# A two-layer encoder on one Trainium2 core: pair products in another order and other bank places, low keys in one tile, weights split in halves, and vector and scalar work held to its order of issue

## The chip, the cores and the metric

The kernel runs on one NeuronCore of a Trainium2 chip. TensorE (PE) multiplies, VectorE (DVE), ScalarE (ACT) and GpSimd (POOL) do the rest, and SyncE (SP) and POOL issue DMAs. Each engine works through its own queue in order; semaphores between queues make one engine wait for another. The metric is the device time of one execution in microseconds (us), lower being better, as the median of three runs.

## The reference

The reference is an encoder trunk of two layers on 512 tokens of width 1024, in float32. Layer 0 is windowed attention with a SwiGLU block, and the diff leaves it alone. Layer 1 is the part that matters here:

```python
def dilated_mixture_attention(h, w_qkv, w_out):
    b, s, _ = h.shape
    qkv = (h @ w_qkv).reshape(b, s, N_GROUPS_B, 3, H_B, HEAD_DIM)
    slopes = alibi_slopes(H_B)[:, None]
    outs, lses = [], []
    for gi, (win, dil) in enumerate(DILATED_GROUPS):
        q = to_residue(qkv[:, :, gi, 0], dil)[:, :, :, None]
        k = to_residue(qkv[:, :, gi, 1], dil)
        v = to_residue(qkv[:, :, gi, 2], dil)
        o, lse = banded_attention(q, k, v, slopes, dil, win // (2 * dil), BLOCK_B)
        outs.append(from_residue(o[:, :, :, 0], b, dil))
        lses.append(from_residue(lse[:, :, :, 0], b, dil))
    wts = jax.nn.softmax(jnp.stack(lses), axis=0)
    o = jnp.einsum('gbsh,gbshd->bshd', wts, jnp.stack(outs).astype(jnp.float32))
    return o.astype(h.dtype).reshape(b, s, H_B * HEAD_DIM) @ w_out
```

It has 16 heads of width 64 in three groups (windows 128, 512 and 2048 with steps 1, 4 and 16), and all queries, keys and values come from one product of the normalised input with `w_qkv`.

## The kernel before

**Precision.** A product of two float32 matrices is made of three matmuls in a reduced float32 type (fp32r): both operands are split into a high part, which ACT copies (`wh`, `xh`, `oh`), and a low part, which DVE subtracts (`wl`, `xl`, `ol`); then high x high, high x low and low x high are added up in a PSUM bank.

**Layer 1** works through pairs of heads, `p` from 0 to 7. For groups 1 and 2 (and group 0 from pair 1 on), the query and key projections of a pair are made together by a scheme of Strassen's kind with seven products instead of eight: `pair_unit(p, g)`. Each product is 12 matmuls of 128 x 128 weights against 256 columns; the line records two half products of six. The products are numbered 1 to 7. Products 1, 2 and 7 run against the normalised input (`xh`, `xl`), the others against sums of it (`oh`, `ol`). Weights 1 and 2 are the two halves of a loaded tile, 6 and 4 those of a tile of sums, and 5, 7 and 3 lie in the buffers `slots`. A unit uses two PSUM banks, `a` and `b`, and in each the halves `one` and `two`. Before, products 1, 5, 6 and 3 pile up in `a[one]`: each adds to what lies there, and between them ACT or DVE reads the place out: after 1 and 5 the gate copies of L1300, after 4 and 3 copies into the keys (L1308, L1314), after 6 an add into the keys (L1311), after 7 the queries (L1318 or L1122).

**Values.** `in_order_values` (group 0) and `value_pair` (groups 1 and 2) make the values. For the first, `value_weights` loads two weight tiles and splits each whole (L115 on ACT, L116 on DVE).

**Attention.** For group 0, `parts(p)` splits queries and keys of a pair. A head's queries `qs[a]` hold the high part in its own 64 partitions and the low part in the other 64. Its keys `ks[a]` hold the high part twice, and `kl[a]` the low part twice (the second time by an ACT copy, L163). `scores_a` then runs for each of two blocks and two heads a matmul with `ks[a]` and one with `kl[a]`, both over 128 partitions: eight matmuls a call, two calls a pair. `scores_b` makes the scores of groups 1 and 2 with 64 partitions a head, the two heads side by side on the array (L1515). `weigh_a` and `weigh_b` weigh the values, in 64 columns a head.

**Order.** PE's order is the order in which the program is written. For ACT and DVE a scheduler sets the order, by readiness as it estimates it. `paced` writes the program of this part: it walks a line of half products (`fill`, made by `lined`) and, at places given by number, issues the steps of attention (`even`, `odd` and their variants for pairs 0 and 1), of normalising the input for the products (`normed`, `operand`, `summed`) and of writing x away (`parked`). `lined` issues the preparations of each unit (loads, sums, splits) at offsets in half products from the unit's first one.

Of the kernel before, what the change touches and what calls it, by code (L numbers as in the profile page):

```python
# [14 lines left out]
S = 512  # L15
# [64 lines left out]
def trunk(ctx, tc, xT, gains, sink, tabs, qsc, wunits, wv, outT, outR):  # L80
# [1014 lines left out]
    with tc.tile_pool(name="l1", bufs=2) as pool:  # L1095
# [102 lines left out]
        def in_order_values(pg):  # L1198
            w, loads, halves = value_weights(1 + 3 * pg)

            def gen():
                if pg:
                    v = pool.tile([128, 4, 256], F32, name="va", bufs=3)
                else:
                    slots["w"] = const.tile([128, NK - 2, S], F32R, name="slots", tag="xb")
                    v = const.tile([128, 4, 256], F32, name="va", tag="xa")
                vals[pg, 0] = v
                yield from v_products(oh, ol, w, v, "ov sc tp mm".split() if pg == 1 else ["mm"] * 4,
                                      lambda b: norm["r"][:, b:b + 1])

            return 16, gen(), [(-11, loads), (-3, lambda: halves(0)), (-2, lambda: halves(1))]

        def pair_unit(p, g):
# [23 lines left out]

            def high(names, src):
                t[names] = [wpool.tile([128, 1024], F32R, name=n) for n in ("wh", "wl")]
                nc.scalar.activation(t[names][0], t[src], AF.Copy)  # L1240

            def low(names, src):
                h, l = t[names]
                nc.vector.tensor_tensor(l, t[src], h.bitcast(F32), op=OP.subtract)
                for k, m in enumerate(names):
                    w[m] = tiles(*[z[:, 512 * k:512 * k + 512] for z in (h, l)])

# [18 lines left out]
            preps = [(-26, sums), (-16, raw), (-8, lambda: high((1, 2), "raw")), (-7, lambda: low((1, 2), "raw")),  # L1266
                     (-5, lambda: add(5)), (-4, lambda: high_one(5)), (-3, lambda: low_one(5)),
                     (-2, lambda: high((6, 4), "sums")), (-1, lambda: low((6, 4), "sums")),
                     (0, lambda: add(7)), (-2, last), (2, lambda: high_one(7)), (3, lambda: low_one(7)),
                     (4, lambda: high_one(3)), (5, lambda: low_one(3))]  # L1270

# [26 lines left out]

            def copied(h):
                nc.scalar.activation(o["gate"][:, (one, two)[h]], o["a"][:, one], AF.Copy, scale=nqs)  # L1300
# [6 lines left out]
            def done4():  # L1307
                nc.scalar.activation(half(o["second"], 1), src(o["b"][:, two]), AF.Copy)  # L1308

            def done6():  # L1310
                nc.vector.tensor_tensor(half(o["second"], 1), src(o["a"][:, one]), half(o["second"], 1), op=OP.add)  # L1311

            def done3():
                nc.scalar.activation(half(o["second"], 0), src(o["a"][:, one]), AF.Copy)  # L1314

# [13 lines left out]
            after = [] if g else list(zip((15, 17, 24, 26), parts(p)))  # L1329
            return 14, products(), preps + after  # L1330

        def value_pair(pg):
# [34 lines left out]
            for m, a in ((1, -5), (2, -2), (5, 2), (4, 6), (6, 10), (7, 14), (3, 18)):  # L1367
                preps += [(a, lambda m=m: high(m)), (a + 1, lambda m=m: low(m))]
            preps += [(1, lambda: add(5)), (9, lambda: add(7))]

# [60 lines left out]
        def scores_a(p, ts):  # L1431
# [6 lines left out]
            for t in ts:  # L1438
                o = tile_a(t)[0]
                for a in range(2):  # L1440
                    out, kp = ps[a][:, o:o + 256], [qk[n, p][a] for n in ("ks", "kl")]
                    if t == 0:
# [5 lines left out]
                    for k in range(2):  # L1448
                        nc.tensor.matmul(out, qk["qs", p][a][:, 128 * t:128 * t + 128], kp[k],  # L1449
                                         start=t == ts[0] and k == 0, stop=k == 1, skip_group_check=True)  # L1450
# [230 lines left out]

        def paced(n, steps, done=0):

            for at, step in sorted((s for s in steps if done <= s[0] < n or s[0] == n == starts[8]), key=lambda s: s[0]):
                spread([at - done, step], fill)
                done = at
            spread([n - done], fill)

# [56 lines left out]
        def x_back():  # L1745
            nonlocal x
            x = stream()
            for j in range(NK):
# [3 lines left out]
                "x01": 43, "x23": 45, "r01": 46, "r23": 48, "back": 57}  # L1752
        odd = {"a01": -12, "xa01": -9, "a23": -8, "xa23": -5, "merge": -4, "t01": 5, "t23": 12, "group": 28,
               "x01": 31, "x23": 37, "r01": 35, "r23": 41, "back": 51}
# [4 lines left out]
        line += [(at, lambda j=j: summed(j)) for j, at in enumerate((50, 52, 54, 56))]  # L1759
        line += [(64 + at, lambda j=j: operand(j)) for at, j in enumerate((4, 5, 6, 7, 0, 1, 2, 3))]  # L1760
        starts = [sum(counts[:p + 1]) for p in range(9)]
        for p in range(8):
            ats = even if p % 2 == 0 else odd
            if p == 0:
                ats = {"a01": -47, "xa01": -44, "a23": -31, "xa23": -28, "merge": -22, "t01": 36, "t23": 44, "group": 56,
                       "x01": 59, "x23": 61, "r01": 63, "r23": 65, "back": 71}
            elif p == 1:
                ats = {**odd, "a01": 13, "xa01": 15, "a23": 16, "xa23": 18, "merge": 19, "t01": 22, "t23": 26}
            steps = attention(p)
# [97 lines left out]
```

## Time and profile before

| | us |
|---|---|
| median of three runs | 1355.34 (1354.69 to 1355.9) |
| the profiled execution, whole | 1357.63 |
| its span, first to last instruction | 1355.8 |
| mean granted TensorE clock | 0.996 |

The value products of layer 1 begin near 522 us and the pair units near 590; the output projection takes over near 963. In the profile's rows, `mm` and `psv` are PSUM banks for products, `sc` for scores, `ov` and `ovb` for weighed values, `tp` for transposes. A row of the timeline has its start, its length, the engine, the line, the operation with the tiles written and read, its shape, the count, and in brackets the engine's idle time before it with what ended it. Successive matmuls overlap: a row of 0.28 us may have its successor start 0.11 us later, so what a matmul takes from the stream is read from the starts. A shape such as 64*128 says that 64 rows and 128 columns of the array are used.

### The profile page before, as it was taken

To read this page: it belongs to the slowest core of one execution; us is meant where nothing else is said; L and a number is where in the kernel's file an instruction comes from. 1 tells how busy PE (TensorE), PEld (TensorE's weight loads), DVE (VectorE), ACT (ScalarE), POOL (GpSimd) and SP (SyncE) were. 2 spreads that over 40 slices of the span, in tenths; PEclk is the share of its full clock that TensorE was granted. 3 is DMA by queue.
4 is the path that set the end of the run, shared out by engine and by line. 5 is a ranking of instruction groups with operands and counts; after the bars stand their busy time and mean duration, and the time that the engine had idled before them with its cause. 6 is when DMAs were issued, how large, how long until landed. Compare 5 with 4: busy or idle time off the path is not lost.

```text
span 1355.8 us, 29663 instructions
## 1 busy us (share of the span) xinstructions
PE 1335.4 (98%) x11874; PEld 1314.5 (97%) x11874; DVE 1071.1 (79%) x1901; ACT 814.5 (60%) x1477; POOL 291.7 (22%) x393
## 2 busy tenths in 40 slices
PE   9999999999999999999999999999999999999997
PEld 9988999999999999998999999999999999999997
DVE  6776558877879999778888788788566887878985
ACT  6776544555555568657777677677444555555553
POOL 1233330121211001023314314313131021210104
PEclk9999999999999999999999999999999999999998
DMA  6110262688765447285556656655245388774821
GB/s 209 63 63 17 78 176 84 178 205 205 185 161 153 135 149 204 71 205 140 148 148 157 151 146 157 155 142 141 102 134 155 111 214 204 187 189 133 199 74 63
DMA packets 86122, 196.36 MB, mean 145 GB/s; under 512 B 11104, under 2 KB 13536, under 8 KB 85984
## 3 DMA queue, kind: packets, MB, share of 16 engines
q1 hardware_dynamic: 63136, 153.42, 35.6%
q0 software_dynamic: 22560, 40.52, 18.3%
q8 instruction: 93, 1.52, 0.5%
q10 hardware_dynamic: 288, 0.52, 0.1%
q14 instruction: 45, 0.37, 0.1%
HBM read 188.59 MB, written 5.84 MB: 143 GB/s over the span
## 4 chain that ended last, share of the span: by engine, by line
PE 82%; ACT 8%; DVE 6%; issue 2%; DMA 1%; POOL 0%; DVEq 0%; SPq 0%; ACTq 0%; POOLq 0%
PE mm L761 18%; PE sc L761 14%; PE mm L144 14%; PE mm L1285 12%; PE psv L144 6%; PE tp L144 6%; PE sc L144 2%; ACT pr L1536 2%; PE ov L467 1%; PE ov L144 1%; DMA w<-wunits 1%; PE sc L1449 1%; ACT pr L443 1%; PE mm L998 1%; DVE pr L436 1%
## 5 line engine op out<-in xcount | busy, mean ns | idle before, releaser
L717 POOL DMA_DIRECT2D w<-wunits x92 | 80.8, 920 | 445.8 <-DMA w<-wunits 145.7
L116 DVE TENSOR_TENSOR wl<-wraw,wh 128x1024 fp32r<-128x1024 f32 (+4 forms) x92 | 98.3, 1078 | 20.9 <-ACT wh L115 18.4
L115 ACT ACTIVATE wh<-wraw 128x1024 fp32r<-128x1024 f32 (+4 forms) x91 | 83.1, 928 | 50.4 <-PE mm L144 40.3
L761 PE MATMUL mm<-bh,wh 128*128 128x256 f32 x368 | 101.6, 276 | 0.0
L761 PE MATMUL mm<-bl,wh 128*128 128x256 f32 x368 | 101.6, 276 | 0.0
L761 PE MATMUL mm<-bh,wl 128*128 128x256 f32 x368 | 101.6, 276 | 0.0
L761 PE MATMUL sc<-bh,wh 128*128 128x256 f32 x368 | 101.6, 276 | 0.0
L761 PE MATMUL sc<-bl,wh 128*128 128x256 f32 x368 | 101.6, 276 | 0.0
L761 PE MATMUL sc<-bh,wl 128*128 128x256 f32 x368 | 101.6, 276 | 0.0
L761 PE MATMUL mm<-bh,h 128*128 128x256 f32 x368 | 101.6, 276 | 0.0
L761 PE MATMUL mm<-bl,h 128*128 128x256 f32 x368 | 101.6, 276 | 0.0
L761 PE MATMUL mm<-bh,l 128*128 128x256 f32 x368 | 101.6, 276 | 0.0
L144 PE MATMUL mm<-xh,wh 128*128 128x256 f32 x384 | 78.3, 286 | 0.4 <-ACT xh L280 0.4
L1285 PE MATMUL mm<-oh,slots 128*128 128x256 f32 x368 | 74.0, 284 | 2.0 <-ACT ssum L1300 1.6
L144 PE MATMUL mm<-xl,wh 128*128 128x256 f32 x384 | 76.0, 280 | 0.0
L144 PE MATMUL mm<-xh,wl 128*128 128x256 f32 x384 | 75.9, 279 | 0.0
L144 PE MATMUL psv<-wl,oh 128*128 128x256 f32 x256 | 72.0, 281 | 2.2 <-DVE wl L116 2.2
L144 PE MATMUL psv<-wh,oh 128*128 128x256 f32 x256 | 72.3, 282 | 0.7 <-ACT v L1393 0.6
L144 PE MATMUL psv<-wh,ol 128*128 128x256 f32 x256 | 71.7, 280 | 0.0
L761 PEld LDWEIGHTS sc<-bl,wh 128*128 128x128 f32 x368 | 69.1, 188 | 0.0
L761 PEld LDWEIGHTS mm<-bl,h 128*128 128x128 f32 x368 | 69.1, 188 | 0.0
L761 PEld LDWEIGHTS mm<-bh,wl 128*128 128x128 f32 x368 | 69.1, 188 | 0.0
(348 smaller groups left out, 5146.8 us busy)
## 6 DMA issues: line engine op xcount, KB each, us to landing
wraw<-wunits SPq DMA_DIRECT2D x122, 512.0 KB, 4.0
w<-wunits SPq DMA_DIRECT2D x207, 256.0 KB, 4.0
w<-wunits POOLq DMA_DIRECT2D x138, 256.0 KB, 6.4
wraw<-wv SPq DMA_DIRECT2D x21, 512.0 KB, 4.6
wraw<-wunits SPq DMA_DIRECT2D x16, 384.0 KB, 4.4
w<-wv SPq DMA_DIRECT2D x8, 512.0 KB, 3.6
w<-wv POOLq DMA_DIRECT2D x8, 512.0 KB, 7.6
xb<-xT SPq DMA_DIRECT2D x6, 256.0 KB, 5.4
```

Source lines behind the costliest of these rows:

```text
L115: nc.scalar.activation(out_h, src, AF.Copy)
L116: nc.vector.tensor_tensor(out_l, src, out_h.bitcast(F32), op=OP.subtract)
L144: nc.tensor.matmul(out[:, cols], a, b[:, cols], start=first and k == 0 and c == 0, stop=last and k == 2, skip_group_check=True)
L436: nc.vector.tensor_tensor_reduce(out=pr[:, e, :w], in0=ps[hf], in1=tab0[:, off:off + w], scale=SLOPES[heads[e]], scalar=-3e38, op0=OP.add, ...
L443: nc.scalar.activation(pr[:, e, :w + 1], pr[:, e, :w + 1], AF.Exp, bias=m[:, 1, e:e + 1], accum_out=m[:, 2, e:e + 1])
L467: nc.tensor.matmul(ov[64 * hf:64 * hf + 64, 256 * n:256 * n + 256], v0[:, k0 // 128 + kb, vs], st["pt", kb][:, 256 * hf:256 * hf + 256], s ...
L717: nc.gpsimd.dma_start(sums[:, 512 * k:512 * k + 512], v[:, 0:512], accum_op=OP.add)
L761: nc.tensor.matmul(out, a[:, j], b[:, j], start=first and j == 0 and i == 0, stop=j == 3 and i == 2, skip_group_check=True)
L998: nc.tensor.matmul(ps[:, 256 * h:256 * h + 256], a, (bl if low else bh)[:, slot, q % 4], start=q == 4 and k == 0 and 256 * h == cols.start ...
L1285: nc.tensor.matmul(out, a[:, j], b[:, j], start=first and j == 0 and i == 0, stop=j == 3 and i == 2, skip_group_check=True)
L1449: nc.tensor.matmul(out, qk["qs", p][a][:, 128 * t:128 * t + 128], kp[k], start=t == ts[0] and k == 0, stop=k == 1, skip_group_check=True)
L1536: nc.scalar.activation(of(pr[:, a, :], c), of(pr[:, a, :], c), AF.Exp, bias=nm[:, c % 2, a:a + 1], accum_out=den[:, c % 2, a:a + 1])
```

## The change

**Keys.** `kl` becomes one tile. Each head's low part stays in its own 64 partitions, the ACT copy L163 goes, and the second matmul of each pair in `scores_a` runs over those 64 partitions, against the high half of the queries alone: the product of the two low parts is left out. In the program the matmul then takes the array as 64 by 128, and the one before and after it as 128 by 128.

```diff
-                    qk["kl", p] = [pool.tile([128, S], F32R, name=f"kl{a}", bufs=1) for a in range(2)]
-                split_keys(qk["k", p, 0], qk["ks", p], qk["kl", p], (a,))
+                    qk["kl", p] = pool.tile([128, S], F32R, name="kl", bufs=1)
+                own, other = (HALVES, HALVES[::-1])[a]
+                k, hi = qk["k", p, 0], qk["ks", p][a]
+                nc.scalar.activation(hi[own], k[own], AF.Copy)
+                nc.scalar.activation(hi[other], hi[own].bitcast(F32), AF.Copy)
+                nc.vector.tensor_tensor(qk["kl", p][own], k[own], hi[own].bitcast(F32), op=OP.subtract)
...
-                    out, kp = ps[a][:, o:o + 256], [qk[n, p][a] for n in ("ks", "kl")]
+                    out, kp = ps[a][:, o:o + 256], [qk["ks", p][a], qk["kl", p][HALVES[a]]]
+                    qp = [qk["qs", p][a], qk["qs", p][a][HALVES[a]]]
...
-                        nc.tensor.matmul(out, qk["qs", p][a][:, 128 * t:128 * t + 128], kp[k],
+                        nc.tensor.matmul(out, qp[k][:, 128 * t:128 * t + 128], kp[k],
```

PE at the first scores of layer 1, before (`psv` is the value product around them):

```order
L144 MATMUL psv<-wh,ol 128x256
L1449 MATMUL sc<-ks_6723,qs_6714 128x256
L1449 MATMUL sc<-kl_6725,qs_6714 128x256
L1449 MATMUL sc<-ks_6724,qs_6715 128x256
L1449 MATMUL sc<-kl_6726,qs_6715 128x256
```

And now:

```order
L144 MATMUL psv<-wh,ol 128x256
L1459 MATMUL sc<-ks_6731,qs_6722 128x256
L1459 MATMUL sc<-kl,qs_6722 128x256
L1459 MATMUL sc<-ks_6732,qs_6723 128x256
L1459 MATMUL sc<-kl,qs_6723 128x256
```

The order is the same; the two `kl` rows read a 64-partition half of one tile each.

**Pair units.** The products run 1, 5, 2, 4, 6, 7, 3 instead of 1, 2, 5, 4, 6, 7, 3. Product 1 goes to `b[two]` and is read by two ACT copies (gate and keys), product 5 opens `a[one]`, 2 goes to `b[one]`, 4 and 7 add to `b[two]`, 6 and 3 to `a[one]`. The copy after product 3 becomes a DVE add.

```diff
             def done1():
                 o["first"], o["second"] = new_q(p, g), new_k(p, g)
                 o["gate"] = o["first"] if g else spool.tile([128, S], F32, name="ssum", bufs=1)
-                copied(0)
+                scaled(0, "b", two)
+                kept(0, "b", two)
...
-                for gen in (product(1, "a", one, True, done1), product(2, "b", one, True, lambda: None),
-                            product(5, "a", one, False, lambda: copied(1)), product(4, "b", two, False, done4),
-                            product(6, "a", one, False, done6), product(7, "b", two, False, done7),
-                            product(3, "a", one, False, done3)):
+                for gen in (product(1, "b", two, True, done1),
+                            product(5, "a", one, True, lambda: scaled(1, "a", one)),
+                            product(2, "b", one, False, lambda: None),
+                            product(4, "b", two, False, lambda: kept(1, "b", two)),
+                            product(6, "a", one, False, lambda: added(1, "a", one)),
+                            product(7, "b", two, False, done7),
+                            product(3, "a", one, False, lambda: added(0, "a", one))):
```

ACT behind the first weighing of values, where the unit of pair 1 and group 0 begins (`acca` is the weighed values, `ssum` the gate copy, `ka` the keys, `mb` and `pr` the exponentials of `scores_b`), before:

```order
L1502 ACTIVATE acca<-ov 128x512
L1536 ACTIVATE pr_7833,mb<-pr_7833,mb 128x2x128 x4
L1300 ACTIVATE ssum<-mm,qs_sb 128x256
L1538 ACTIVATE mb<-mb 128x4
L1536 ACTIVATE pr_7851,mb<-pr_7851,mb 128x2x128 x4
L1538 ACTIVATE mb<-mb 128x4
L1300 ACTIVATE ssum<-mm,qs_sb 128x256
```

And now:

```order
L1512 ACTIVATE acca<-ov 128x512
L1546 ACTIVATE pr_7845,mb<-pr_7845,mb 128x2x128 x4
L1308 ACTIVATE ssum<-mm,qs_sb 128x256
L1311 ACTIVATE ka<-mm 128x8x32
L1548 ACTIVATE mb<-mb 128x4
L1546 ACTIVATE pr_7863,mb<-pr_7863,mb 128x2x128
L1308 ACTIVATE ssum<-mm,qs_sb 128x256
```

Four exponentials still stand ahead of the first gate copy. The key copy follows it at once, and the second gate copy has moved ahead of three more exponentials.

**Weights.** The splits of the tiles of products 1 and 2 and of 6 and 4 are made in halves of 512 columns (`high` and `low` with a half `k`), at offsets of their own.

```diff
-            def high(names, src):
-                t[names] = [wpool.tile([128, 1024], F32R, name=n) for n in ("wh", "wl")]
-                nc.scalar.activation(t[names][0], t[src], AF.Copy)
+            def high(names, src, k):
+                if names not in t:
+                    t[names] = [wpool.tile([128, 1024], F32R, name=n) for n in ("wh", "wl")]
+                cols = slice(512 * k, 512 * k + 512)
+                nc.scalar.activation(t[names][0][:, cols], t[src][:, cols], AF.Copy)
...
-            return 16, gen(), [(-11, loads), (-3, lambda: halves(0)), (-2, lambda: halves(1))]
+            return 16, gen(), [(-15, loads), (-7, lambda: halves(0)), (-2, lambda: halves(1))]
```

**Order of issue.** `paced` now marks, after each half product, the newest ACT and the newest DVE instruction, and what is issued from the third half product on may not be ordered ahead of the mark on its engine. Some offsets of attention steps change too (for odd pairs `merge` from -4 to 0, `x01` from 31 to 34, `x23` from 37 to 39, and a few of pairs 0 and 1).

```diff
+            for c in range(n + 1):
+                with ExitStack() as held:
+                    for mark in marks[c - 3] if c >= 3 else ():
+                        held.enter_context(tc.issue_after(mark))
+                    for step in at.get(c, ()) if c < n else [f for s, f in steps if s == n == starts[8]]:
+                        step()
+                    if c < n:
+                        next(fill)
+                marks.append([newest(e) for e in (mybir.EngineType.Activation, mybir.EngineType.DVE,)])
```

DVE during the group 0 values, from the low half of one unit's first weight tile on (`wl` are the low halves of value weights, L1711 and its successor L1732 normalise the input, L1717 to L1719 make sums of it), before:

```order
L116 TENSOR_TENSOR wl<-wraw,wh 128x1024
L1711 SCALAR_TENSOR_TENSOR v_6667<-xb,g_sb,rb 128x512
L1711 SCALAR_TENSOR_TENSOR v_6668<-xb,g_sb,rb 128x512 x2
L1717 TENSOR_TENSOR k_6661<-k_6661 128x256
L116 TENSOR_TENSOR xl<-v_6667,xh 128x512 x2
L116 TENSOR_TENSOR xl<-v_6668,xh 128x512 x2
L1718 TENSOR_TENSOR k_6661<-v_6667,k_6661 128x256
L1717 TENSOR_TENSOR k_6662<-k_6662 128x256
L1719 SCALAR_TENSOR_TENSOR v_6667<-k_6661,v_6667 128x256
L116 TENSOR_TENSOR wl<-wraw,wh 128x1024
```

And now:

```order
L116 TENSOR_TENSOR wl<-wraw,wh 128x1024
L116 TENSOR_TENSOR xl<-v_6667,xh 128x512
L116 TENSOR_TENSOR wl<-wraw,wh 128x1024
L1732 SCALAR_TENSOR_TENSOR v_6667<-xb,g_sb,rb 128x512
L1468 ISA pr_7003,mx_7012<-sc,tab_6509 128x256
```

The second subtraction follows the first after one other row; before, three rows of normalising, four low parts and four sums stood between them.

More of the change, by code (lines that the diff above doesn't have):

```diff
@@ L1236, in tiles, with low @@
                 return [z.rearrange("p (j c) -> p j c", j=4) for z in (h, l)]
-            def high(names, src):
-                t[names] = [wpool.tile([128, 1024], F32R, name=n) for n in ("wh", "wl")]
[L1240 to L1246, printed above, removed]
+            def high(names, src, k):
[3 more added lines that the diff above has]
+                nc.scalar.activation(t[names][0][:, cols], t[src][:, cols], AF.Copy)
+            def low(names, src, k):
+                h, l = [z[:, 512 * k:512 * k + 512] for z in t[names]]
+                nc.vector.tensor_tensor(l, t[src][:, 512 * k:512 * k + 512], h.bitcast(F32), op=OP.subtract)
+                w[names[k]] = tiles(h, l)
             def one_of(m):
@@ L1264, in add @@
                 nc.vector.tensor_tensor(out, t["sums"][:, 512:1024] if m == 5 else one_of(5)[2], out, op=OP.add)
[L1266 to L1270, printed above, removed]
+            first, later = ((1, 2), "raw"), ((6, 4), "sums")
+            preps = [(-26, sums), (-16, raw), (-8, lambda: high(*first, 0)), (-7, lambda: low(*first, 0)),
+                     (-7, lambda: add(5)), (-6, lambda: high_one(5)), (-4, lambda: low_one(5)),
+                     (-4, lambda: high(*first, 1)), (-3, lambda: low(*first, 1)), (-1, lambda: add(7)),
+                     (-2, lambda: high(*later, 1)), (-1, lambda: low(*later, 1)),
+                     (-1, lambda: high(*later, 0)), (-1, lambda: low(*later, 0)),
+                     (-2, last), (2, lambda: high_one(7)), (3, lambda: low_one(7)),
+                     (2, lambda: high_one(3)), (3, lambda: low_one(3))]
             def against(m):
@@ L1297, in src, with scaled, kept, added @@
                 return of_class(z, 8) if g == 0 else z
-            def copied(h):
-                nc.scalar.activation(o["gate"][:, (one, two)[h]], o["a"][:, one], AF.Copy, scale=nqs)
+            def scaled(h, key, cols):
+                nc.scalar.activation(o["gate"][:, (one, two)[h]], o[key][:, cols], AF.Copy, scale=nqs)
+            def kept(h, key, cols):
+                nc.scalar.activation(half(o["second"], h), src(o[key][:, cols]), AF.Copy)
+            def added(h, key, cols):
+                nc.vector.tensor_tensor(half(o["second"], h), src(o[key][:, cols]), half(o["second"], h), op=OP.add)
             def done1():
@@ L1304, in done1 @@
                 o["gate"] = o["first"] if g else spool.tile([128, S], F32, name="ssum", bufs=1)
-                copied(0)
[L1307 to L1314, printed above, removed]
+                scaled(0, "b", two)
+                kept(0, "b", two)
             def done7():
@@ L1368, in value_pair @@
                 preps += [(a, lambda m=m: high(m)), (a + 1, lambda m=m: low(m))]
-            preps += [(1, lambda: add(5)), (9, lambda: add(7))]
+            preps += [(1, lambda: add(5)), (8, lambda: add(7))]
             def product(m, key, first, post):
@@ L1680, in lined, with newest, paced @@
                 yield
[L1682 to L1687, printed above, removed]
+        def newest(engine):
+            return next(i for i in reversed(nc.cur_bb.bb.instructions) if i.engine == engine)
+        def paced(n, steps):
+            at, marks = {}, []
+            for c, step in sorted(steps, key=lambda s: s[0]):
+                at.setdefault(max(c, 0), []).append(step)
+            for c in range(n + 1):
[7 more added lines that the diff above has]
+                marks.append([newest(e) for e in (mybir.EngineType.Activation, mybir.EngineType.DVE,)])
         norm["by class"] = pool.tile([128, S], F32, name="acca", bufs=1)
@@ L1752, in trunk @@
                 "x01": 43, "x23": 45, "r01": 46, "r23": 48, "back": 57}
-        odd = {"a01": -12, "xa01": -9, "a23": -8, "xa23": -5, "merge": -4, "t01": 5, "t23": 12, "group": 28,
-               "x01": 31, "x23": 37, "r01": 35, "r23": 41, "back": 51}
+        odd = {"a01": -12, "xa01": -9, "a23": -8, "xa23": -5, "merge": 0, "t01": 5, "t23": 12, "group": 28,
+               "x01": 34, "x23": 39, "r01": 35, "r23": 41, "back": 51}
         ats, line, begin = [], [], 0
@@ L1758, in trunk @@
         line += [(at, lambda j=j: normed(j)) for j, at in enumerate((18, 20, 22, 24, 26, 35, 37, 39))]
-        line += [(at, lambda j=j: summed(j)) for j, at in enumerate((50, 52, 54, 56))]
-        line += [(64 + at, lambda j=j: operand(j)) for at, j in enumerate((4, 5, 6, 7, 0, 1, 2, 3))]
+        line += [(at, lambda j=j: summed(j)) for j, at in enumerate((50, 52, 55, 56))]
+        line += [(63 + at, lambda j=j: operand(j)) for at, j in enumerate((4, 5, 6, 7, 0, 1, 2, 3))]
         starts = [sum(counts[:p + 1]) for p in range(9)]
@@ L1764, in trunk @@
             if p == 0:
[L1765 to L1766 removed]
+                ats = {"a01": -45, "xa01": -44, "a23": -31, "xa23": -28, "merge": -22, "t01": 34, "t23": 44, "group": 56,
+                       "x01": 59, "x23": 61, "r01": 63, "r23": 65, "back": 68}
             elif p == 1:
[L1768 removed]
+                ats = {**odd, "a01": 13, "xa01": 15, "a23": 16, "xa23": 18, "merge": 19, "t01": 19, "t23": 28}
             steps = attention(p)
```

2 lines of the change are left out of this document (1 added, 1 removed).

## The prediction

> **What bounds the kernel now.** I read the page's busy times and chain first, then the stretch table around the part that the diff touches, then the waits of TensorE there.
>
> ```profile
> span 1355.8 us, 29663 instructions
> ...
> PE 1335.4 (98%) x11874; PEld 1314.5 (97%) x11874; DVE 1071.1 (79%) x1901; ACT 814.5 (60%) x1477; POOL 291.7 (22%) x393
> ...
> PE 82%; ACT 8%; DVE 6%; issue 2%; DMA 1%; POOL 0%; DVEq 0%; SPq 0%; ACTq 0%; POOLq 0%
> ...
> 522.00:590.00 68.00, 65.76 (x561) 65.32 (x560) 55.61 (x99) 43.47 (x79) 7.22 (x11) 0.97 0.44 122
> 590.00:980.00 390.00, 383.93 (x3655) 375.29 (x3655) 319.14 (x726) 271.46 (x602) 111.02 (x152) 1.00 0.59 150
> ```
>
> TensorE bounds it, with 98% of the span. The last two rows are the value products (522 to 590 us) and the pair units with attention (590 to 980); columns are PE, PEld, DVE, ACT and POOL busy, then clock and DMA. DVE works 319 of 390 us there and ACT 271, so neither is full; they matter only where TensorE waits for one instruction of theirs. These are all such waits from 519 to 985 us (total idle, times, longest):
>
> ```profile
> PE mm L1285 <- ACT q L1300: 2.7, 5, 0.6
> PE psv L144 <- DVE wl L116: 2.2, 2, 1.9
> PE mm L1285 <- ACT ssum L1300: 1.6, 4, 0.5
> PE sc L1449 <- DVE sta L1461: 0.7, 1, 0.7
> PE psv L144 <- ACT v L1393: 0.6, 2, 0.3
> ```
>
> So 7.8 us of idle time is what another order could win at the most directly. A wait costs more than its idle time, as one of the four ssum waits shows:
>
> ```profile
> 619.48 0.49 ACT L1536 ACTIVATE pr<-pr,mb 128x256 f32<-128x256 f32 x1
> ...
> 619.97 0.45 ACT L1300 ACTIVATE ssum<-mm,qs_sb 128x256 f32<-128x256 f32 x1
> ...
> 619.81 0.28 PE L1285 MATMUL mm<-xh,wl 128*128 128x256 f32 x1
> 620.48 0.38 PE L1285 MATMUL mm<-oh,slots 128*128 128x256 f32 x1 [0.39 <-ACT ssum L1300]
> 620.70 0.28 PE L1285 MATMUL mm<-ol,slots 128*128 128x256 f32 x1
> ```
>
> Product 5 adds into the place that product 1 left and ACT must first copy out; ACT does the exponentials before that copy. The matmuls start 0.67 and then 0.22 us apart, where undisturbed ones start 0.115 apart (rows below). That is 0.66 us lost for 0.39 shown, so 0.27 more than the view says: the restart.
>
> **Term 1, pair units: minus 6.7 us.** Now product 5 opens a bank place of its own, product 4 follows product 1 with two products between, and product 6 follows 5 with two between instead of one. The nine L1300 waits are those of 5 for the first copy and of 6 for the second. Two products are 24 matmuls, 2.8 us at 0.115. In the place above, four exponentials end at 619.97, the two copies that product 4 needs then take 0.45 and up to 0.62 (the ka row of L1308 below), till about 621.1; product 4 would begin at 617.08 plus 36 times 0.115, 621.2. So they just fit, and elsewhere ACT is less laden. Gain: 2.7 + 1.6 + 9 x 0.27 = 6.7. Bounds: nothing, if the binding order only puts other work ahead of the copies, and 8.8 if the L1449 and L1393 waits (0.7 + 0.6 + 3 x 0.27 = 2.1) go too. I take 6.7, since distances and not luck remove it. What is late next is product 7, still one product behind the copy after 4, and product 3 behind the add after 6; both keep their small waits.
>
> **Term 2, value products: minus 4.3 us.**
>
> ```profile
> 549.20 0.41 DVE L1719 SCALAR_TENSOR_TENSOR v<-k,v 128x256 f32<-128x256 f32 x1
> 549.53 1.21 DVE L116 TENSOR_TENSOR wl<-wraw,wh 128x1024 fp32r<-128x1024 f32 x1
> ...
> 548.61 0.28 PE L144 MATMUL psv<-wh,oh 128*128 128x256 f32 x1
> 550.79 0.38 PE L144 MATMUL psv<-wl,oh 128*128 128x256 f32 x1 [1.90 <-DVE wl L116]
> ...
> 552.07 0.42 PE L144 MATMUL psv<-wh,ol 128*128 128x256 f32 x1
> ...
> 555.27 0.35 PE L144 MATMUL psv<-wh,ol 128*128 128x256 f32 x1
> ```
>
> The low half of a value weight stands on DVE behind sums that nobody needs yet. TensorE idles 1.90 us and then, from 552.07 to 555.27, runs 15 matmul steps of 0.213 us: half speed. In the new order three normalised tiles, three of their low parts and all sums stand behind this subtraction instead of ahead of it. Two waits are 2.2 + 2 x 0.27 = 2.7; the half-speed stretch costs 16 x 0.10 = 1.6. Together 4.3; bounds nothing and 4.3. I take 4.3, since DVE reaches it earlier by that much work. The value loads move four half products earlier on SP's queue together with their first split, so their lead of eight steps stays (8 x 6 x 0.115 = 5.5 us, against the landing below); what they pass are the writes of parked x, read back only at the end.
>
> **Term 3, scores: plus 25.6 us.** The low keys now exist for 64 rows only, so every second of the eight matmuls of a call works on a 64 by 128 part of the array and its neighbours on the whole. Three places bound the price:
>
> ```profile
> 639.82 0.28 PE L1449 MATMUL sc<-ks,qs 128*128 128x256 f32 x1
> 639.93 0.28 PE L1449 MATMUL sc<-kl,qs 128*128 128x256 f32 x1
> ...
> 705.98 0.28 PE L1285 MATMUL mm<-ol,slots 128*128 128x256 f32 x1
> 706.10 0.28 PE L1285 MATMUL mm<-oh,slots 128*128 128x256 f32 x1
> 706.31 0.49 PE L1515 MATMUL sc<-k,q 64*128 64x128 f32 x4
> ...
> 616.87 0.28 PE L1515 MATMUL sc<-k,q 64*128 64x128 f32 x2
> 617.08 0.38 PE L1285 MATMUL mm<-xh,wh 128*128 128x256 f32 x1
> 617.30 0.28 PE L1285 MATMUL mm<-xl,wh 128*128 128x256 f32 x1
> 617.41 0.29 PE L1285 MATMUL mm<-xh,wl 128*128 128x256 f32 x1
> ...
> 23.58 0.39 PE L144 MATMUL mm<-xh,wl 128*128 128x256 f32 x2
> 23.80 0.95 PE L298 MATMUL ssq<-ones,ssum 128*128 128x1 f32 x8
> ```
>
> Alike, they start 0.11 apart. Into the 64-row form the step is 0.21 instead of 0.115, and the second pair of the four starts 0.49 - 0.28 = 0.21 after the first, not 0.11: 0.10 for emptying the array and 0.10 for weights that could not be loaded ahead. Out of it the same: 0.21, then 0.22. The last two rows change to plain f32 but keep the whole array: two matmuls and on in 0.22, no loss. So it is the shape that costs, 0.20 us per change. Sixteen calls with four low matmuls each, entered and left: 128 changes, 25.6 us, and nothing hides it on the engine that is the bound. Ends: nothing, as in the first two rows, and 25.6. I take 25.6, as the nearest rows are changes of just this shape, though between f32r and f32, never within f32r.
>
> The Trainium skill, "TensorEngine Tiling (Array Packing)", section Tiling Modes, says that changing the tiling mode drains the TensorE; it says nothing of the weights. By the drain alone this term would be 128 x 0.095 = 12.2, by the rows it is 25.6.
>
> **Terms at nothing.**
>
> ```profile
> L163 ACT ACTIVATE kl<-kl 64x512 fp32r<-64x512 f32 x14 | 8.8, 631 | 0.3
> L1308 ACT ACTIVATE ka<-mm 128x256 f32<-128x256 f32 x7 | 4.3, 620 | 2.8 <-PE mm L1285 2.8
> L1255 ACT ACTIVATE slots<-w 128x512 fp32r<-128x512 f32 x22 | 13.9, 630 | 19.9 <-PE mm L1285 18.7 <-issue 1.2
> L1240 ACT ACTIVATE wh<-w 128x1024 fp32r<-128x1024 f32 x23 | 24.3, 1057 | 13.1 <-PE mm L1285 9.2 <-ACT q L1300 2.1 <-PE psv L144 1.7
> ...
> L1259 DVE TENSOR_TENSOR slots<-w,slots 128x512 fp32r<-128x512 f32 x22 | 15.1, 688 | 1.5 <-ACT slots L1255 1.2
> L1244 DVE TENSOR_TENSOR wl<-w,wh 128x1024 fp32r<-128x1024 f32 x23 | 28.9, 1256 | 5.5 <-ACT wh L1240 5.3
> L1311 DVE TENSOR_TENSOR ka<-mm,ka 128x256 f32<-128x256 f32 x7 | 4.4, 623 | 0.2
> ...
> wraw<-wv SPq DMA_DIRECT2D x21, 512.0 KB, 4.6
> ```
>
> ACT loses 16 copies of 0.63 (10.1 us) and gains 46 splits in two (46 x (2 x 0.63 - 1.06) = 9.2). DVE gains 46 x (2 x 0.69 - 1.26) = 5.5 and 23 adds of at most 0.62, 14.3: 20 us on 319 of 390. The idle rest hides it; if it didn't, each late add would cost product 3 at most its 0.62 plus 0.27, so 0 to 20 us in all, and I take nothing as weights are ready steps ahead. The order edges add no wait between engines. But ACT and DVE now may stand at an instruction whose input is late, with the copies that TensorE wants behind it: that is the lower end of term 1.
>
> **Sum.** The profiled execution took 1357.63 us, 1.8 around its span. 1357.6 - 6.7 - 4.3 + 25.6 = 1372.2. It was 2.3 above the median of the runs, so 1369.9: **1370 us**, own range 1362 to 1377.
>
> **Rivals.** *Shape changes cost nothing within f32r* (faster): 1357.6 - 11.0 - 2.3 = 1344. For it: no row here changes shape between f32r matmuls. Against: the f32 control lost nothing without a change of shape. It decides from below 11.0 / 128 = 0.086 us per change. The Trainium skill, "TensorE: Matmul & The Clock Gate", section Why this matters for your kernels, says a single matmul of few rows takes as long as one of 128; by that alone this rival would hold. No row here shows such a matmul between whole ones. *Only the emptying counts*, 0.21 - 0.115 = 0.095 a change, since weights for the other shape load meanwhile: 1357.6 - 11.0 + 128 x 0.095 - 2.3 = 1356.5. Against: both 0.21 steps and the 0.22. *No wait goes*, since the bound order puts ACT and DVE behind late inputs, or since 1.6 idle us in each 2.5 us call halve the clock as 1.9 idle us did at 552: 1357.6 + 25.6 - 2.3 = 1381.
>
> **How the numbers follow.** Forecast 0.62, free changes 0.18, emptying alone 0.12, no wait goes 0.08. The range 1344 to 1380 leaves out about half of the second and of the last, 0.13. A measurement can tell 0.2%, 2.7 us. Faster: 0.18 and a third of the 0.12, 0.22. Same: 0.05 of the 0.12. Slower: the rest, 0.73.
>
> **What would show it.** Right: scores matmuls (new line L1459) starting 0.3 apart, 2.5 us a call instead of 0.9; no TensorE wait for the gate copies of the pair units; no half-speed stretch near 552. Wrong: scores still 0.11 apart, which gives 1344, or new waits of TensorE for DVE adds.

## The result, and the profile after

The changed kernel takes 1378.8 us (median), the one before 1355.6, six runs each: a ratio of **1.0168, 95% interval 1.0151 to 1.0185**, or 23 us more. The profiled execution of the changed kernel took 1376.65 us, 19.0 more than the profiled one of before. Below, a ratio to the kernel before is also given in us of 1355.5, since the runs on each chip were compared with runs of before on that chip.

First the page of the changed kernel (span, busy times), then its stretches of the value products and of the pair units (PE, PEld, DVE, ACT and POOL busy, clock, DMA):

```profile
span 1374.9 us, 29681 instructions
...
PE 1353.2 (98%) x11874; PEld 1318.0 (96%) x11874; DVE 1085.6 (79%) x1970; ACT 807.0 (59%) x1507; POOL 298.8 (22%) x393
```

```profile
522.00:590.00 68.00, 68.00 (x573) 65.95 (x573) 57.03 (x100) 43.48 (x79) 7.69 (x11) 1.00 0.42 119
590.00:980.00 390.00, 382.28 (x3452) 362.30 (x3453) 321.30 (x759) 258.19 (x610) 116.22 (x145) 1.00 0.58 145
```

TensorE executes the same 11874 matmuls in 19 us more. In the value products it no longer idles and the clock is full; in the unit stretch it is as busy as before but gets through 3452 matmuls where it did 3655: the matmuls themselves have become dearer. The scores show where, in TensorE's timeline of one call:

```profile
644.95 0.28 PE L1459 MATMUL sc<-ks,qs 128*128 128x256 f32 x1
645.16 0.38 PE L1459 MATMUL sc<-kl,qs 64*128 64x256 f32 x1
645.47 0.38 PE L1459 MATMUL sc<-ks,qs 128*128 128x256 f32 x1
...
647.34 0.39 PE L1293 MATMUL mm<-oh,slots 128*128 128x256 f32 x1
647.57 0.28 PE L1293 MATMUL mm<-ol,slots 128*128 128x256 f32 x1
```

The step into the 64-row form is 0.21, every further one 0.31, and the first matmul behind the call takes 0.23. A call lasts 2.39 us (647.34 - 644.95) plus 0.11 behind it; before, eight steps of 0.114. That is 1.59 us a call and 25.4 for sixteen. The loads of the weights (PEld) for the first three matmuls of this call show what a change does:

```profile
644.84 0.19 PEld L1459 LDWEIGHTS sc<-ks,qs 128*128 128x128 f32 x1
645.15 0.18 PEld L1459 LDWEIGHTS sc<-kl,qs 64*128 64x128 f32 x1
645.47 0.19 PEld L1459 LDWEIGHTS sc<-ks,qs 128*128 128x128 f32 x1
```

Ahead of the first scores matmul, which has the shape of the one before it, the weights begin to load 0.11 us before the matmul (644.84, 644.95). At each change the load begins only with its matmul (645.15 and 645.16, then 645.47 and 645.47). So by these rows some 0.10 of the 0.20 us a change is the load that no longer runs ahead; the other 0.10 passes before the load begins.

TensorE's waits from 500 to 1030 us, in the changed kernel (total, times, longest):

```profile
PE mm L1293 <- DVE k L1314: 2.1, 4, 0.7
PE tp L1572 <- POOL pr L1560: 2.0, 3, 0.8
PE mm L1293 <- ACT k L1311: 1.7, 3, 0.6
PE sc L1459 <- ACT ks L1149: 1.5, 1, 1.5
PE mm L1293 <- ACT mb L1548: 0.9, 1, 0.9
PE mm L1293 <- DVE ka L1314: 0.6, 3, 0.2
```

None of the waits of before is left, and there are 8.8 us of others in 15 places, where there were 7.8 in 14. So the stages have to be measured apart. These rows (of the views by line: count, shortest/median/longest ns, first and last start) give the first matmul of L998, a line that both kernels share and that first runs ahead of the value products, and the first and the last of the pair units, for before and for the changed kernel:

```profile
L998 PE MATMUL mm<-bh,wh x40: 276/276/365, 498.9 to 1344.6; 128*128 128x256 f32 x40
L1285 PE MATMUL mm<-xh,wh x184: 276/278/384, 592.0 to 950.6; 128*128 128x256 f32 x184
L1285 PE MATMUL mm<-oh,slots x368: 276/281/388, 594.8 to 957.9; 128*128 128x256 f32 x184
```

```profile
L998 PE MATMUL mm<-bh,wh x40: 276/276/367, 500.0 to 1364.0; 128*128 128x256 f32 x40
L1293 PE MATMUL mm<-xh,wh x184: 276/276/385, 591.7 to 970.9; 128*128 128x256 f32 x184
L1293 PE MATMUL mm<-oh,slots x368: 276/281/388, 593.1 to 977.2; 128*128 128x256 f32 x184
```

In both kernels the two stretches hold the same numbers of matmuls, 780 and 3384. From the first L998 to the first unit matmul: 93.1 us before, 91.7 now, though two dearer scores calls (3.2 us) lie inside; without them 88.5, so **4.6 us were won in the value products**. From the first unit matmul to the last: 365.9 before, 385.5 now, with fourteen dearer calls (22.3 us); without them 363.2, so **only 2.7 were won in the units**. Which edit won these is a question for the experiments below.

Two of the new waits in detail. The timeline around product 2 of a unit:

```profile
675.18 0.62 ACT L1260 ACTIVATE slots<-w 128x512 fp32r<-128x512 f32 x1
...
675.63 0.28 PE L1293 MATMUL mm<-oh,slots 128*128 128x256 f32 x1
675.70 0.46 ACT L1308 ACTIVATE q<-mm,qs_sb 128x256 f32<-128x256 f32 x1
...
676.06 0.37 ACT L1311 ACTIVATE k<-mm 128x256 f32<-128x256 f32 x1
...
676.49 0.38 PE L1293 MATMUL mm<-xh,wh 128*128 128x256 f32 x1 [0.58 <-ACT k L1311]
```

Product 5 issues its last matmul at 675.63. Product 2, which writes `b[one]`, starts at 676.49, right behind the end (676.43) of the key copy, which reads `b[two]`. The order of the program has it so: the first matmul of product 2 (the first row below) carries a wait for ACT; the first of product 4 (the last row), which writes the place that was read, carries none.

```
3971 L1293 MATMUL mm_7550<-xh_6277,wh_7480 128x256 [waits Activation_49]
...
3985 L1293 MATMUL mm_7550<-oh_6507,wh_7526 128x256
```

The wait goes by bank, not by half. The Trainium skill, "PSUM — Partial Sum Buffer", section PSUM bank collisions raise a hardware error, says to guard PSUM by bank and quadrant and not by address; this program guards by bank, and the 0.58 us are the price of that here. What an unguarded access would do, no run here shows.

And the add after product 6, on VectorE and then TensorE:

```profile
681.93 1.29 DVE L1575 STREAM_TRANSPOSE pt<-pr 128x512 f32<-128x512 f32 x2
683.15 0.64 DVE L1617 TENSOR_TENSOR acca<-rrow,acca 128x512 f32<-128x512 f32 x1
683.73 0.40 DVE L1314 TENSOR_TENSOR k<-mm,k 128x256 f32<-128x256 f32 x1
```

```profile
683.26 0.28 PE L1293 MATMUL mm<-xh,slots 128*128 128x256 f32 x1
684.18 0.39 PE L1293 MATMUL mm<-oh,slots 128*128 128x256 f32 x1 [0.64 <-DVE k L1314]
```

The add stands behind two transposes and a product of the attention, and product 3 waits for it.

### The profile page after: what moved, and what is told of

Read it like the earlier page. It is cut to its first block, busy times and chain, and to the rows that moved or that the text cites. A ratio compares the mean times of both kernels' runs of the same rounds, so it can differ in the third digit from the quotient of the medians.

```text
span 1374.9 us, 29681 instructions
## 1 busy us (share of the span) xinstructions
PE 1353.2 (98%) x11874; PEld 1318.0 (96%) x11874; DVE 1085.6 (79%) x1970; ACT 807.0 (59%) x1507; POOL 298.8 (22%) x393
## 4 chain that ended last, share of the span: by engine, by line
PE 86%; DVE 8%; ACT 4%; issue 1%; DMA 0%; POOL 0%; DVEq 0%; SPq 0%; ACTq 0%; POOLq 0%
PE mm L761 18%; PE sc L761 14%; PE mm L144 13%; PE mm L1293 12%; PE psv L144 9%; PE tp L144 6%; PE sc L1459 3%; PE sc L144 2%; PE ov L467 1%; PE ov L144 1%; PE ovb L1585 1%; PE sc L1525 1%; DVE wl L1250 1%; PE tp L1487 1%; ACT pr L443 1%
## 5 line engine op out<-in xcount | busy, mean ns | idle before, releaser
L116 DVE TENSOR_TENSOR wl<-wraw,wh 128x1024 fp32r<-128x1024 f32 (+4 forms) x92 | 99.2, 1088 | 22.8 <-ACT wh L115 20.3
L1560 POOL TENSOR_SCALAR pr<-pr,mb 128x256 f32<-128x256 f32 x64 | 53.1, 846 | 89.6 <-DVE mb L1553 55.3
L761 PEld LDWEIGHTS mm<-bh,wh 128*128 128x128 f32 x368 | 69.1, 188 | 0.0
```

Source lines behind the costliest of these rows:

```text
L116: nc.vector.tensor_tensor(out_l, src, out_h.bitcast(F32), op=OP.subtract)
L761: nc.tensor.matmul(out, a[:, j], b[:, j], start=first and j == 0 and i == 0, stop=j == 3 and i == 2, skip_group_check=True)
L1560: nc.gpsimd.tensor_scalar(of(pr[:, a, :], c), of(pr[:, a, :], c), den[:, c % 2, a:a + 1], 1.0, op0=OP.mult, op1=OP.mult)
```

## The experiments

**1. Is it the shape?** Four kernels. In the first the changed kernel has its full low keys back (and with them the product of the two low parts):

```diff
-                    qk["kl", p] = pool.tile([128, S], F32R, name="kl", bufs=1)
+                    qk["kl", p] = [pool.tile([128, S], F32R, name=f"kl{a}", bufs=1) for a in range(2)]
+                split_keys(qk["k", p, 0], qk["ks", p], qk["kl", p], (a,))
```

> The changed kernel with the two 128-row low-key tiles and the second copy on ScalarE back, nothing else undone. Theory (each change of array shape between fp32r matmuls costs 0.20 us, 128 of them): 25.6 us less than the changed kernel's 1378.8, so about 1353; scores matmuls again 0.11 apart, 0.91 us a call. Rival (the loss comes from the new waits of the pair units and from the binding order, the shapes are cheap): above 1370. Either way the seven-odd microseconds of waits before product 2 and product 3 should still be there, since nothing of the units is touched.

Measured: 1365.52 us, ratio 1.0076 (1.0058 to 1.0094), 10.3 above before: between theory and rival. The scores are back at 0.11, but they wait:

```profile
PE sc L1454 <- ACT kl L163: 5.8, 4, 2.4
PE sc L1454 <- DVE sta L1466: 2.8, 3, 1.0
```

The second copy of the low keys, costed at nothing in the prediction, is late in the changed order, and so is what follows it.

The second has the key part of the diff alone on the kernel before.

> The kernel before with only the low keys of 64 rows. Theory (shapes, 0.20 us a change): 1355.4 + 25.6 = 1381, and the waits for the gate copies (4.3 us idle) stay. Rival (the price arises only together with the new order of the units): under 1365. If 1381 holds, all the rest of the change together is worth only 1381 - 1379 = about 2 us where the prediction had 11.

Measured: 1375.11, ratio 1.0147 (1.0131 to 1.0164), 19.9 above before and 6 below the theory; no wait for value weights is left in it, though nothing of them was touched. All the rest of the change then adds 22.8 - 19.9 = 2.9 us instead of taking 11 away; as the two intervals overlap, it may also add nothing. The profiled execution of this kernel takes 91.8 us from the first L998 to the first unit matmul (500.0 to 591.8) and 385.6 from there to the last (977.4), as the changed kernel does (91.7 and 385.5), though its units, weights and order of issue are those of before. So the 2.7 us above can't be put down to the new order of the units.

The third and fourth keep the 64-row keys and change only the order of the eight matmuls of a call:

```diff
-            for t in ts:
-                o = tile_a(t)[0]
-                for a in range(2):
...
-                    for k in range(2):
+            for k, t, a in [(k, t, a) for k in range(2) for t in ts for a in range(2)]:
```

```diff
+            for k, t, a in [(k, t, a) for t in ts for k in range(2) for a in range(2)]:
```

> The changed kernel with the eight matmuls of a scores call in another order: the four whole-array ones first, then the four of 64 rows. 2 changes of shape a call instead of 8, so 32 instead of 128. Theory (the change of shape is what costs, 0.20 us each): 96 x 0.20 = 19.2 less, 1359.6; if the two heads' 64-row matmuls also run side by side, two steps of 0.115 a call less, 3.7 more, 1356. Rival (a 64-row matmul in fp32r is itself slow, 0.5 us, in whatever order): 1379, no change.

> The same with the grouping inside each block: two whole-array matmuls, two of 64 rows, four times a change of shape a call, 64 in all. Theory (0.20 us a change): 64 x 0.20 = 12.8 less than the changed kernel, 1366; with side by side heads as much as 3.7 less, 1362: halfway between the changed kernel and the run grouped by call, so the time should be linear in the number of changes. Rival (slow matmul, not change): 1379.

Measured: 1357.29, ratio 1.0014 (1.0003 to 1.0024), and 1364.74, ratio 1.0067 (1.0052 to 1.0083). Both lie in the range of the theory; the slow matmul is refuted. TensorE's timeline of a call grouped as a whole:

```profile
682.71 0.62 PE L1456 MATMUL sc<-ks,qs 128*128 128x256 f32 x4
683.25 0.50 PE L1456 MATMUL sc<-kl,qs 64*128 64x256 f32 x4
683.68 0.38 PE L1293 MATMUL mm<-oh,slots 128*128 128x256 f32 x1
683.90 0.28 PE L1293 MATMUL mm<-ol,slots 128*128 128x256 f32 x1
```

The call lasts 0.97 us (682.71 to 683.68) instead of 2.39. Eight of the sixteen calls last 0.97 to 0.99, seven 1.03 to 1.26, and one, with a wait of 1.5 in it, 2.72. Four 64-row matmuls, of two heads on the two halves of the array, take 0.43 with the change out of the form in it.

**2. Where did the gain of the units go, and what took the value waits away?** Four kernels. The value offsets alone, on the kernel before:

```diff
-            return 16, gen(), [(-11, loads), (-3, lambda: halves(0)), (-2, lambda: halves(1))]
+            return 16, gen(), [(-15, loads), (-7, lambda: halves(0)), (-2, lambda: halves(1))]
```

> The kernel before with only the new offsets of the group 0 value weights (loads 15, first splits 7 ahead instead of 11 and 3). Theory of the prediction's second term (the low half of a value weight must only be taken earlier): both waits of the value products and the half-clock stretch go, 4.3 us, 1355.6 - 4.3 = 1351. Rival (the wait is decided by where the scheduler puts the sums on VectorE, which the 64-row keys alone already changed in the second run, and not by these offsets): within 1 us of the kernel before, with a wait of the same size left or moved.

Measured: ratio 1.0003 (0.9994 to 1.0012), no difference. The waits are all there:

```profile
PE psv L144 <- DVE wl L116: 2.2, 2, 2.0
```

The kernel before with 64-row keys and scores grouped by call (the diffs of the second and third run):

> The kernel before with the 64-row low keys and the scores grouped by call, units and order of issue as before. From the run with the keys alone (1375.1) grouping should take what it took from the changed kernel, 21.5 us: 1354. If the pair units, weights and order of issue of the change are worth the 6.7 us of the prediction's first term, this must lie 6 us above the grouped changed kernel (1357.3), at 1364; if the gain went into new waits, at or below it.

Measured: 1356.61, ratio 1.0008 (0.9999 to 1.0017); the changed kernel grouped had 1.0014 (1.0003 to 1.0024). The two agree within their intervals, so the whole rest of the change brings nothing that can be measured: the 6.7 us of the units are refuted.

The changed kernel, grouped, with the splits and the turning back out of the way of the copies and the add:

```diff
-                     (-2, last), (2, lambda: high_one(7)), (3, lambda: low_one(7)),
-                     (2, lambda: high_one(3)), (3, lambda: low_one(3))]
+                     (-2, last), (4, lambda: high_one(7)), (5, lambda: low_one(7)),
+                     (6, lambda: high_one(3)), (7, lambda: low_one(3))]
...
-               "x01": 34, "x23": 39, "r01": 35, "r23": 41, "back": 51}
+               "x01": 34, "x23": 39, "r01": 35, "r23": 41, "back": 54}
```

> The changed kernel with grouped scores, and two places by number moved: the splits of the weights of products 7 and 3 two to four half products later (they stand ahead of the two copies after product 1 on ScalarE), and the turning back of odd pairs from 51 to 54 (its two transposes and the product with the row sums stand on VectorE ahead of the add after product 6). Theory (product 2 waits for the key copy after product 1 because both lie in bank b, and the copy is late by the two splits; product 3 waits for an add that is late by the turning back): the three waits of 0.58 and the three of 0.64 us go, with 0.27 each for the restart 5.3 us, 1357.3 - 5.3 = 1352. Rival (the engines are so full that the wait moves on to the next instruction): 1356 to 1358.

Measured: 1360.42, ratio 1.0035 (1.0023 to 1.0047), above even the rival. The waits aimed at are gone, the key copy's from the list and the add's down to two of 0.5 in all; the scores now wait instead:

```profile
PE sc L1456 <- DVE kl L1150: 1.6, 3, 0.5
```

In the timeline, VectorE's product of the turning back and the low keys behind it, and the scores that wait for these:

```profile
682.34 0.64 DVE L1614 TENSOR_TENSOR acca<-rrow,acca 128x512 f32<-128x512 f32 x1
...
683.01 0.69 DVE L1150 TENSOR_TENSOR kl<-ka,ks 64x512 fp32r<-64x512 f32 x1
...
683.75 0.50 PE L1456 MATMUL sc<-kl,qs 64*128 64x256 f32 x3 [0.53 <-DVE kl L1150]
```

The cause named for each wait was right, and removing it won nothing: what was moved back now stands ahead of the low keys, which the scores want.

The changed kernel, grouped, without the marks:

```diff
-                    for mark in marks[c - 3] if c >= 3 else ():
-                        held.enter_context(tc.issue_after(mark))
```

> The changed kernel with grouped scores and without the marks that hold ScalarE and VectorE to the order of issue. Theory (the new waits come from the bank that product 2 shares with the copies and from the places of the splits, not from the marks): the waits of product 2 stay and the time is within 3 us of 1357.3. Rival (the marks put late work ahead of the copies): the waits of product 2 and 3 go, up to 12 us, 1346.

Measured: 1359.98, ratio 1.0034 (1.0022 to 1.0046), 2.7 above the same kernel with marks. Product 2 waits more (4.5 us in 8 places, where the kernel with marks has 2.6 in 4), now mostly behind exponentials, product 3 no less (3.2 us, where it has 2.7), and value waits are back:

```profile
PE mm L1293 <- ACT mb L1545: 3.5, 4, 0.9
PE mm L1293 <- DVE k L1314: 2.0, 3, 0.7
PE psv L144 <- DVE wl L116: 1.8, 2, 1.0
```

So in the changed kernel the marks don't make the new waits of products 2 and 3.

**3. Everything but the shape.** The low keys of a head lie in a tile of 128 rows of its own, whose other 64 rows are zeroed once. The sums are those of the changed kernel (no product of the low parts, no second copy), and every matmul keeps the whole array. On the kernel before, on the changed kernel, and, as a third kernel, the marks alone on the kernel before (the `paced` diff shown ahead of the prediction). The diff of the zeroed tiles:

```diff
+                if ("kl", 0) not in qk:
+                    qk["kl", 0] = [pool.tile([128, S], F32R, name=f"kl{h}", bufs=1) for h in range(2)]
+                    for h in range(2):
+                        nc.gpsimd.memset(qk["kl", 0][h][HALVES[1 - h]].bitcast(F32), 0.0)
+                qk["kl", p] = qk["kl", 0]
...
+                nc.vector.tensor_tensor(qk["kl", p][a][own], k[own], hi[own].bitcast(F32), op=OP.subtract)
```

> The kernel before with the change's low keys (each head's in its own 64 partitions, no second copy, the product of the two low parts left out) in two tiles whose other 64 partitions are zeroed once, so that all scores matmuls keep the whole array. Theory (128 changes of shape cost 25.6 us, and the copies' absence helped the rest): the run with the 64-row keys alone took 1375.1, so 1375.1 - 25.6 = 1349.5, with a call of 0.91 us and the value waits gone as there. Rival (dropping the copies is worth nothing, and the value waits come and go with the order that the scheduler happens to make): 1355.5.

> The changed kernel with the same zeroed tiles: everything of the change but the change of shape. Theory: 1378.8 - 25.6 = 1353, with scores calls of 0.91 us; the run with full low keys, at 1365.5, lost its other 12 us to TensorE waiting for the second copy of the low keys (5.8 us idle) and for what followed it. Rival (those 12 us come from scores that now arrive earlier than their keys, with or without the copy): 1360 to 1365, with waits of the scores for the low keys.

> The kernel before with only the marks that hold ScalarE and VectorE to the order of issue. Theory (what the prediction put to offsets in the value products was done by the marks: they keep later sums from passing a weight's subtraction): both value waits and the half-clock stretch go, 4.4 us, 1355.5 - 4.4 = 1351, and the gate-copy waits stay. Rival (marks put late work ahead of the copies that TensorE wants): 1358 or more. If the value waits stay, the offsets and the marks are needed together, or it was the keys.

Measured: on the kernel before 1354.38, ratio **0.9982** (0.9974 to 0.9991), a small gain of 2.4 us where 6 were expected; a value wait of 1.4 us stays, which is a part of what is missing. On the changed kernel 1356.67, ratio **1.0001** (0.9990 to 1.0012): 22.6 us below the changed kernel, and no different from before. The marks alone: 1362.17, ratio 1.0039 (1.0027 to 1.0051): 5.3 us slower, as the rival had it, with value waits left and a new one of the scores:

```profile
PE sc L1449 <- ACT ks L161: 2.0, 1, 2.0
PE psv L144 <- DVE wl L116: 1.5, 2, 0.9
```

A call on the zeroed tiles of the changed kernel, its first and its last matmul, is eight starts within 0.85 us:

```profile
639.08 0.28 PE L1462 MATMUL sc<-ks,qs 128*128 128x256 f32 x1
...
639.93 0.28 PE L1462 MATMUL sc<-kl,qs 128*128 128x256 f32 x1
```

The kernels with 64-row keys and with zeroed rows differ in their matmuls by the shape alone, and there are two such pairs: 1.0168 - 1.0001 on the changed kernel and 1.0147 - 0.9982 on the one before, 22.6 and 22.4 us.

The two kernels with zeroed rows have the same keys and no change of shape in `scores_a`, so between them the rest of the change can be seen stage by stage. The first and the last matmul of the pair units, in the old order and in the new:

```profile
L1293 PE MATMUL mm<-xh,wh x184: 276/276/384, 591.6 to 948.3; 128*128 128x256 f32 x184
L1293 PE MATMUL mm<-oh,slots x368: 276/281/388, 594.4 to 955.6; 128*128 128x256 f32 x184
```

```profile
L1297 PE MATMUL mm<-xh,wh x184: 276/281/388, 587.0 to 948.8; 128*128 128x256 f32 x184
L1297 PE MATMUL mm<-oh,slots x368: 276/281/386, 588.4 to 955.1; 128*128 128x256 f32 x184
```

The units take 364.0 us in the old order and 368.1 in the new; from the first L998 (499.1 and 498.4) to the first unit matmul it is 92.5 and 88.6. In these two executions the new order loses 4.1 us in the units and wins 3.9 in the value products.

**4. What is worth keeping.** The zeroed tiles and the value offsets on the kernel before, and the marks for the value products only:

```diff
+                    for mark in marks[c - 3] if 3 <= c < starts[0] else ():
```

> The kernel before with the zeroed low-key tiles of the ninth run, the new offsets of the value weights, and the marks for the value products alone (not from the pair units on). Theory (offsets and marks are each too little, and together they take the value waits away): the one value wait that the ninth run kept, 1.43 us, goes with 0.27 for its restart, and the pair units keep the waits of the ninth run, so 2.4 + 1.7 = 4.1 us below the kernel before, about 1351.5. Rival (the wait moves into the pair units, as in the run with the copies moved ahead): 1353 to 1356.

Measured: 1351.94, ratio **0.9968** (0.9956 to 0.9980), 4.3 us below before: the theory's 4.1, and faster than both kernels. One value wait of 0.5 is left of the 1.4; the units keep the waits of old:

```profile
PE mm L1293 <- ACT q L1308: 3.5, 5, 0.9
PE mm L1293 <- ACT ssum L1308: 1.6, 4, 0.5
PE psv L144 <- DVE wl L116: 0.5, 1, 0.5
```

## Why the prediction was right, and where not

The sign, the chief term and its size were right: 1370 forecast, 1378.8 measured, inside the range to 1380 but above the forecast's own range to 1377. That it lies inside is in part luck: of the 11 us of terms 1 and 2 nothing is left in the whole time, and the shape cost 3 us less than its rows. The prediction's signs came out mixed: the scores matmuls start 0.31 apart, no wait for the gate copies and no half-speed stretch is left, but the new waits for DVE adds, its sign of being wrong, are there too. Step by step:

**Term 3, the scores (+25.6): right.** The rows give 25.4. Changes of shape cost inside fp32r what they cost between fp32r and f32, so the rivals "free" and "only the emptying" fall. By the emptying alone a step would be 0.21, and the steps are 0.31, since the weights don't load meanwhile. The Trainium skill ("TensorEngine Tiling (Array Packing)", section Tiling Modes) says that a change of the tiling mode drains TensorE; the trace agrees that each change holds TensorE up, but no row shows whether the 0.10 us before the load are this drain. In the whole kernel the shape costs 22.5 us, 3 less than the rows. While TensorE is held up in a call, the other engines catch up: with the shape gone from the changed kernel, a wait of 1.7 us for a key copy appears that it doesn't have:

```profile
PE mm L1297 <- ACT ka L1315: 1.7, 1, 1.7
```

That this is the whole of the 3 us was not shown.

**Term 2, the value products (-4.3): right in size, its ground half right.** 4.6 were won, and 3.9 between the two kernels with zeroed rows; both waits and the half-speed stretch are gone. The new offsets alone win nothing, and with the marks alone 1.5 us of those waits stay; with both they go, as they did in every kernel that had both but the last, where 0.5 stays. The keys alone removed them too. The prediction read the order that came out, which was enough; it could not have said which edit made it.

**Term 1, the units (-6.7): wrong.** In the profiled execution 2.7 were won, but as much with the units of before and 64-row keys; between the two kernels with zeroed rows the new order loses 4.1. The step that failed is "product 4 follows product 1 with two products between". Product 2 is one of these two, lies in the same bank, and takes the wait for the copies itself, with one product between and two copies to wait for instead of one. The second failure is that product 7 and product 3 "keep their small waits": before, all nine listed waits of the units are those of products 5 and 6, and 7 and 3 have none; now product 3 has seven, up to 0.65 and 2.7 us in all, the longest behind attention work on VectorE, and product 2 has four, 2.6 in all. Together that is 5.3 where the nine were 4.3. The bound of nothing was in the prediction for another reason, the binding order. For the waits of products 2 and 3 that reason is refuted, as they stay without the marks; but the marks alone made the kernel before 5.3 us slower, so they cost something there, and how much of the 4.1 is theirs stays open.

**Terms at nothing: the second copy of the low keys was not nothing in the new order.** The full low keys, 10.3 above before, and the zeroed ones, 0.1 above, differ in ScalarE's work by this copy: 10.2 us, and the scores' waits for it and for what follows it, 8.6 us, are in the one kernel and not in the other. On the kernel before, the zeroed tiles without the copy won 2.4 in all. So the idle rest of ScalarE hid this copy in the old order, where the scores had no wait for it, and not in the new.

**The conversion to a median (-2.3): wrong.** The profiled execution of before lay above its median, that of the changed kernel 2.2 below. These 4.5 us and the 4.0 missing in term 1 are nearly the whole of the 8.8 between 1370 and 1378.8. Why the changed kernel's executions spread from 1375 to 1380 stays open.

**The rival "no wait goes"** forecast 1381, nearer to 1378.8 than the 1370 of the prediction, but not by what happened: the old waits did go, and new ones came. Its half clock fell too: the granted clock is 1.00 in both stretches, in spite of the gaps in the scores.

## What to carry to other kernels

Here a matmul that uses half the rows of the array was not cheaper among whole ones: each change of shape cost about 0.2 us, and a zeroed other half, which keeps the shape, was worth 22 us. Where that can't be had, put all matmuls of one shape together: that took about 21 us off the changed kernel. When a wait is to be removed by distance, count from the next write to the same PSUM bank, not to the same address, if the program's waits go by bank as they do here. And with one engine busy for 98% of the span, moving work on the others to remove its waits mostly made the next ones: 7.8 us of idle time were exchanged for 8.8.

## What was unexpected in the hardware

A change of the array's shape costs TensorE about 0.20 us between matmuls of 0.113, and half of this is the load of weights that begins only with its matmul, as the rows of the changed kernel's call show.

Two 64-row matmuls in fp32r on the two halves of the array ran side by side: four of them took 0.43 us in the grouped call, with a change of shape in it, where four in turn with whole ones between took 2.39 with their partners. The Trainium skill, "TensorEngine Tiling (Array Packing)", section Tiling Modes, says that tiles work independently, and the row agrees. Still the zeroed rows, which waste half of the array, were a little faster: on the kernel before, 15 of 16 calls take 0.91 to 0.94 us to the next matmul with them and 0.97 to 0.99 grouped, with another 0.11 behind the grouped call.
